# One subtraction on GpSimd, one exponential and one sum in place of eight exponentials, in the compressed branch of a two-layer decoder

## The chip, the cores and the metric

The kernel runs on one core of a Trainium2 chip. Its engines run side by side, each through a queue of its own, in order: TensorE (PE in the profile; PEld is its loading of weights), VectorE (DVE), ScalarE (ACT), GpSimd (POOL) and SyncE (SP), which issues the transfers. An instruction that needs another engine's result waits on a semaphore, and what stands behind it in its queue waits too. The metric is device time in microseconds (us), as the median of several runs.

## The reference, cut to what matters

Layer 1 is native sparse attention. Its compressed branch lets each of 16 heads (4 groups of 4) attend to 63 compressed key blocks; the probabilities also choose which blocks the second branch reads.

```python
    lg_c = jnp.einsum('bsgrd,bcgd->bgrsc', q, kc).astype(jnp.float32) * scale
    mask_c = cmp_end[None, :] <= pos[:, None]
    p_c = jax.nn.softmax(jnp.where(mask_c, lg_c, NEG), axis=-1)
    p_c = jnp.where(mask_c, p_c, 0.0)
    o_c = jnp.einsum('bgrsc,bcgd->bsgrd', p_c.astype(vc.dtype), vc)
    ...
    imp = jnp.einsum('bgsc,cj->bgsj', p_c.sum(axis=2), overlap)
    ...
    imp = jnp.where(forced, FORCE, jnp.where(causal, imp, -1.0))
    _, idx = lax.top_k(imp, n_sel)
```

## The kernel before, in words

The sequence of 1024 positions is cut into eight tiles of 128. Layer 0 comes first, then the projections of layer 1, with which the compressed branch is interleaved, then the attention of layer 1 and the output layer.

The compressed branch is worked in 16 units, here called unit 0 to unit 15 in their order. A unit (`cmp_unit`) is one group of four heads by two tiles of positions, so it has eight rows of 64 scores on each of 128 partitions. `cmp_main` walks through nine steps; step n issues the two units of a group g and half s (n = 2g + s), and between them the transposes (`ptc`) and value matmuls (`oc`) of the step before. The score matmuls of a unit (L1043) write the tile `sc`, of which there is one; VectorE adds the mask and the two halves of the scores (L1052, L1053), and from then on `sc` is free for the next unit. The scores are negated, so VectorE takes minima (L1054) where a softmax takes maxima. ScalarE makes eight exponentials (L1056), one for each row, since each row has its own bias; each also gives the row's sum. VectorE takes reciprocals (L1057). In the first half (s = 0) they are multiplied by the gate (L1068) and GpSimd applies them (L1070). In the second half VectorE normalizes (L1063), sums over heads (L1066), GpSimd applies the gate (L1070), and VectorE chooses blocks in small steps on 128x32 elements (L1074 to L1081).

The names of units in the queues are `cL_s_u`, `cP_s_u`, `cs_s_u`: unit 0 is `0_0`, unit 1 `0_1`, unit 2 `1_0`, unit 3 `1_1`, and the next group begins again.

`merge` runs this main line together with a filler, the projections that are left (`nsa_fill`, `nsa_zs`: the tiles `pn_v`, `pn_ka`, `pn_kr`, `nz`): after a piece of the main line it takes pieces of filler by their stated costs. That sets the order on TensorE. Each section of weights comes in by a transfer, VectorE makes its high part (`whi`, L128) and GpSimd the low part (`wlo`, L129, 128x1024). The transposes' results are split by ScalarE (`pth`, L147) and VectorE (`ptl`, L148). On the other engines the order is set by the scheduler of the program builder, which sees the dependences; it is fixed when the kernel is built.

Of the kernel before, what the change touches and what calls it, by code (L numbers as in the profile page):

```python
# [13 lines left out]
AF = mybir.ActivationFunctionType  # L14
OP = mybir.AluOpType
AX = mybir.AxisListType
# [5 lines left out]
P = 128  # L22
# [18 lines left out]
def tile_fox_nsa(ctx, tc, a, out):  # L41
    nc = tc.nc
    V, A, G, T = nc.vector, nc.scalar, nc.gpsimd, nc.tensor
# [993 lines left out]
    def cmp_unit(g, s, u, Q):  # L1037
        nm = f"{g}_{s}_{u}"
        kcm = ready["kcm"]
        sc = psC.tile([P, 2, 512], F32, tag="sc", name=f"sc_{nm}")  # L1040
        for y in range(2):
            for r in range(4):
                T.matmul(sc[:, y, r * P:(r + 1) * P], Q[r][:, (2 * u + y) * P:(2 * u + y + 1) * P],  # L1043
                         kcm[:, g].rearrange("p a c -> p (a c)"), start=True, stop=True)
        sc = sc.rearrange("p y (r a c) -> p y r a c", r=4, a=2)
        t0 = 4 * s + 2 * u
        L = pc[0].tile([P, 2, 4, 64], F32, tag="cL", bufs=2, name=f"cL_{nm}")
        Pc = pc[0].tile([P, 2, 4, 64], F32, tag="cP", bufs=4, name=f"cP_{nm}")
        sm = pc[0].tile([P, 3, 8], F32, tag="cs", bufs=3, name=f"cs_{nm}")
        L8 = L.rearrange("p y r c -> p (y r) c")  # L1050
        P8 = Pc.rearrange("p y r c -> p (y r) c")
        V.tensor_tensor(L, sc[:, :, :, 1, :], cmask[:, t0:t0 + 2, None, :].to_broadcast([P, 2, 4, 64]), OP.add)  # L1052
        V.tensor_tensor(L, sc[:, :, :, 0, :], L, OP.add)  # L1053
        V.tensor_reduce(sm[:, 0, :], L8, AX.X, OP.min)  # L1054
        for i in range(8):
            A.activation(P8[:, i, :], L8[:, i, :], AF.Exp, bias=sm[:, 0, i:i + 1], scale=-1.0, accum_out=sm[:, 1, i:i + 1])  # L1056
        V.reciprocal(sm[:, 2, :], sm[:, 1, :])  # L1057
        if t0 == 0:
            V.tensor_scalar(sm[:, 2, 0:4], sm[:, 2, 0:4], crow, None, OP.mult)
        ri = sm[:, 2, :].rearrange("p (y r) -> p y r", y=2)  # L1060
        gc = gates[:, t0:t0 + 2, 12 * g:12 * g + 12:3]
        if s:
            V.tensor_tensor(P8, P8, sm[:, 2, :, None].to_broadcast([P, 8, 64]), OP.mult)  # L1063
            pcs = pc[0].tile([P, 2, 65], F32, tag="pcs", bufs=2, name=f"pcs_{nm}")
            G.memset(pcs[:, :, 0:1], 0.0)
            V.tensor_reduce(pcs[:, :, 1:65], Pc.rearrange("p y r c -> p y c r"), AX.X, OP.add)  # L1066
        else:
            V.tensor_tensor(ri, ri, gc, OP.mult)  # L1068
            gc = ri
        G.tensor_tensor(Pc, Pc, gc[:, :, :, None].to_broadcast([P, 2, 4, 64]), OP.mult)  # L1070
        if s:
            im = pc[0].tile([P, 2, 16], F32, tag="im", bufs=2, name=f"im_{nm}")
            mx = pc[0].tile([P, 2, 8], F32, tag="mx", bufs=2, name=f"mx_{nm}")
            V.tensor_reduce(im, pcs[:, :, 1:65].rearrange("p y (j c) -> p y j c", c=4), AX.X, OP.add)  # L1074
            V.tensor_tensor(im, im, pcs[:, :, 0:64:4], OP.add)
            V.tensor_tensor(im, im, impt[:, 0, 2 * u:2 * u + 2, :], OP.mult)
            V.tensor_tensor(im, im, impt[:, 1, 2 * u:2 * u + 2, :], OP.add)
            for y in range(2):
                V.max(mx[:, y, :], im[:, y, :])
                V.match_replace(im[:, y, :], mx[:, y, :], im[:, y, :], -2.0)  # L1080
            V.tensor_scalar(selb[:, g, 2 * u:2 * u + 2, :], im, -2.0, BIG, OP.not_equal, OP.mult)  # L1081
        return Pc

    def cmp_main():
# [17 lines left out]
        for n in range(9):  # L1102
            cur = []
            if n < 8:
                g, s = divmod(n, 2)
                yield lambda g=g: ("q", g // 2) in ready and "gates" in ready
                if n == 0:
                    Qs[n] = [load_q(pc[0], r, 0, 8) for r in range(4)]
                    yield 2500
                cur.append(cmp_unit(g, s, 0, Qs[n]))  # L1110
                yield 900
# [3 lines left out]
            if n < 8:  # L1115
                cur.append(cmp_unit(g, s, 1, Qs.pop(n)))
                if n < 7 and ("q", (n + 1) // 4) in ready:
                    Qs[n + 1] = [load_q(pc[0], 4 * ((n + 1) // 2) + r, (n + 1) % 2, 8) for r in range(4)]
                yield 900
                if n < 7 and n + 1 not in Qs:  # L1120
                    yield lambda n=n: ("q", (n + 1) // 4) in ready
                    Qs[n + 1] = [load_q(pc[0], 4 * ((n + 1) // 2) + r, (n + 1) % 2, 8) for r in range(4)]
# [76 lines left out]
    bias = []  # L1199
# [264 lines left out]
```

## Time and profile before

| what | value |
|---|---|
| median of 3 runs | 1553.28 us (1551.8 to 1553.96) |
| the profiled execution | 1553.53 us |
| its span in the profile | 1551.7 us |
| mean granted TensorE clock | 0.967 |
| TensorE busy | 1434.4 us (92%) |
| VectorE busy | 1063.7 us (69%) |
| ScalarE busy | 803.3 us (52%) |
| GpSimd busy | 556.5 us (36%) |
| score matmuls of the compressed branch | 837.3 to 966.5 us |

A profile is one execution; its times count from the start of the span. Busy time is the time with an instruction at work, and idle time is put down to what ended it. The compressed branch takes about a tenth of the span.

### The profile page before, as it was taken

To read this page: it belongs to the slowest core of one execution; us is meant where nothing else is said; L and a number is where in the kernel's file an instruction comes from. 1 tells how busy PE (TensorE), PEld (TensorE's weight loads), DVE (VectorE), ACT (ScalarE), POOL (GpSimd) and SP (SyncE) were. 2 spreads that over 40 slices of the span, in tenths; PEclk is the share of its full clock that TensorE was granted. 3 is DMA by queue.
4 is the path that set the end of the run, shared out by engine and by line. 5 is a ranking of instruction groups with operands and counts; after the bars stand their busy time and mean duration, and the time that the engine had idled before them with its cause. 6 is when DMAs were issued, how large, how long until landed. Compare 5 with 4: busy or idle time off the path is not lost.

```text
span 1551.7 us, 29460 instructions
## 1 busy us (share of the span) xinstructions
PE 1434.4 (92%) x10488; PEld 1188.4 (77%) x10488; DVE 1063.7 (69%) x2756; ACT 803.3 (52%) x2025; POOL 556.5 (36%) x604
## 2 busy tenths in 40 slices
PE   5999999999999787999999979899898998888898
PEld 4888888888787666878888768687787877667686
DVE  6586878778787755457364687787686777678433
ACT  5364646545555643233133655566565666567321
POOL 1232323222233500043241342557647657345300
PEclk9999999999999889999999999999999999899899
DMA  7796767867878756343345586757756856674642
GB/s 263 223 183 146 163 155 156 172 160 149 178 156 174 166 104 231 95 133 96 126 134 176 149 202 179 206 123 151 168 122 143 195 118 137 151 167 113 161 138 95
DMA packets 405763, 242.72 MB, mean 156 GB/s; under 512 B 332464, under 2 KB 353840, under 8 KB 405360
## 3 DMA queue, kind: packets, MB, share of 16 engines
q1 hardware_dynamic: 405616, 240.84, 63.5%
q8 instruction: 83, 1.36, 0.4%
q14 instruction: 64, 0.52, 0.1%
HBM read 120.96 MB, written 44.11 MB: 106 GB/s over the span
## 4 chain that ended last, share of the span: by engine, by line
PE 61%; DVE 16%; ACT 6%; DMA 6%; POOL 6%; issue 4%; SPq 1%; POOLq 0%; DVEq 0%; ACTq 0%
PE S_n L1256 4%; DVE P_n L1263 3%; PE y L133 3%; PE y L135 3%; PE y L134 3%; POOL hl_n L1270 3%; PE ptp_n L1288 2%; PE v L133 2%; PE v L135 2%; PE v L134 2%; PE S L579 2%; PE S L580 2%; PE q L133 2%; PE O L613 2%; PE k L133 2%
## 5 line engine op out<-in xcount | busy, mean ns | idle before, releaser
L1266 ACT ACTIVATE P_n<-P_n,m_n 128x640 f32<-128x640 f32 (+7 forms) x256 | 187.0, 731 | 74.6 <-DVE m_n L1265 37.3
L1256 PE MATMUL S_n<-nk,nq 128*128 128x320 f32 (+5 forms) x768 | 189.0, 356 | 19.4 <-DVE m_n L1263 18.6
L597 ACT ACTIVATE P<-P,m 128x512 f32<-128x512 f32 (+1 forms) x192 | 116.9, 610 | 133.2 <-DVE m L588 132.3
L568 POOL TENSOR_TENSOR Bd<-B,tri 128x128 f32<-128x128 f32 x128 | 62.3, 501 | 245.3 <-DVE m L588 228.5
L1263 DVE CUSTOM_DVE_ANT_0 P_n<-S_n,wmask 128x128 f32<-128x128 f32 (+1 forms) x192 | 113.5, 598 | 53.4 <-POOL hl_n L1270 37.7
L1256 PEld LDWEIGHTS S_n<-nk,nq 128*128 128x128 f32 x768 | 125.2, 194 | 32.3 <-DVE m_n L1263 23.3
L1270 POOL TENSOR_TENSOR hl_n<-P_n,hl_n 128x640 f16<-128x640 f32 (+4 forms) x128 | 141.5, 1109 | 7.5
L599 DVE SCALAR_TENSOR_TENSOR hl<-P,hl 128x512 f16<-128x512 f32 (+1 forms) x192 | 124.1, 664 | 21.8 <-ACT hl L598 20.7
L150 ACT ACTIVATE pth_n<-ptp_n 128x512 f16<-128x512 f32 (+1 forms) x160 | 86.6, 546 | 76.1 <-PE ptp_n L1288 75.4
L1288 PE MATMUL ptp_n<-ident,P_n 128*128 128x128 f32 x576 | 98.2, 292 | 19.3 <-DVE ptl_n L151 10.3
L151 DVE SCALAR_TENSOR_TENSOR ptl_n<-ptp_n,pth_n 128x512 f16<-128x512 f32 (+1 forms) x160 | 100.5, 634 | 20.8 <-ACT pth_n L150 20.1
L1269 POOL CAST hl_n<-P_n 128x640 f16<-128x640 f32 (+4 forms) x128 | 74.1, 584 | 98.7 <-ACT P_n L1266 78.4
L133 PE MATMUL y<-wo,ohi 128*128 128x512 f32 x240 | 96.8, 403 | 8.0 <-ACT ohi L693 8.0
L1288 PEld LDWEIGHTS ptp_n<-ident,P_n 128*128 128x128 f32 x576 | 71.3, 149 | 33.1 <-DVE ptl_n L151 11.9
L134 PE MATMUL y<-wo,ohi 128*128 128x512 f32 x240 | 96.0, 400 | 0.0
L135 PE MATMUL y<-wo,olo 128*128 128x512 f32 x240 | 94.9, 398 | 0.9 <-DVE olo L694 0.9
L598 ACT ACTIVATE hl<-P 128x512 f16<-128x512 f32 (+1 forms) x192 | 92.5, 513 | 4.3 <-DMA pT<-hl 2.8
L1296 PE MATMUL O_n<-nv,pth_n 128*128 128x64 f16 x576 | 76.1, 199 | 3.7 <-ACT pth_n L150 3.7
L579 PE MATMUL S<-KH,Q 128*128 128x512 f32 (+1 forms) x192 | 68.8, 372 | 10.6 <-DVE m L588 10.4
L1297 PE MATMUL O_n<-nv,pth_n 128*128 128x64 f16 x576 | 74.9, 197 | 0.0
L1298 PE MATMUL O_n<-nv,ptl_n 128*128 128x64 f16 x576 | 72.2, 197 | 0.0
L1296 PEld LDWEIGHTS <-pth_n 128*128 128x128 f16 x576 | 53.8, 101 | 21.4 <-ACT pth_n L150 9.1
(384 smaller groups left out, 4517.0 us busy)
## 6 DMA issues: line engine op xcount, KB each, us to landing
nq<-qD SPq DMA_DIRECT2D x64, 256.0 KB
B<-cD SPq DMA_DIRECT2D x16, 512.0 KB
wo<-wD SPq DMA_DIRECT2D x16, 512.0 KB
nq<-qD SPq DMA_DIRECT2D x64, 128.0 KB
of<-oF SPq DMA_DIRECT2D x12, 512.0 KB
x<-in_x_dram SPq DMA_DIRECT2D x8, 512.0 KB
wst_k<-in_fox_w_dram SPq DMA_DIRECT2D x8, 512.0 KB
wst_v<-in_fox_w_dram SPq DMA_DIRECT2D x8, 512.0 KB
```

What stands on the lines that cost most here:

```text
L133: T.matmul(ps, wh, mh, start=first, stop=False, **kw)
L134: T.matmul(ps, wh, ml, start=False, stop=False, **kw)
L135: T.matmul(ps, wl, mh, start=False, stop=last, **kw)
L151: V.scalar_tensor_tensor(lo[:, 0:n], pt[:, 0:n], scale, h, OP.mult, OP.subtract)
L597: A.activation(L[:, 0:n], L[:, 0:n], AF.Exp, bias=init, scale=-1.0, accum_out=self.lr[:, col + c:col + c + 1])
L599: V.scalar_tensor_tensor(lo[:, cs], L[:, 0:n], UP, hi[:, cs], OP.mult, OP.subtract)
L1256: T.matmul(ps[:, b, 0:w], self.q[x][:, qi * P:(qi + 1) * P], k[:, k0 + b * w:k0 + b * w + w], start=(x == 0), stop=(x == 1))
L1263: V.tensor_tensor_reduce(dst, src, mk, 1.0, 3e38, OP.add, OP.min, m)
L1266: A.activation(L, L, AF.Exp, bias=m, scale=-1.0, accum_out=self.l[:, y, qi:qi + 1])
L1270: G.tensor_tensor(hl[:, n:2 * n], L, hl[:, 0:n], OP.subtract)
L1288: T.transpose(pt[:, (x + i) * P:(x + i + 1) * P], L[:, kb * P - k0:(kb + 1) * P - k0], ident)
L1296: T.matmul(o, hi, v[:, 0:64], start=first, stop=False)
```

## The change

In each unit GpSimd subtracts the minima from all eight rows in place, in one instruction whose second operand is the minimum spread over 64 elements; ScalarE then makes one exponential of 128x512 elements, without bias and without sums; and VectorE makes the sums of the rows in one reduction. The rest of the program text is the same.

```diff
         V.tensor_reduce(sm[:, 0, :], L8, AX.X, OP.min)
-        for i in range(8):
-            A.activation(P8[:, i, :], L8[:, i, :], AF.Exp, bias=sm[:, 0, i:i + 1], scale=-1.0, accum_out=sm[:, 1, i:i + 1])
+        G.tensor_tensor(L8, L8, sm[:, 0, :, None].to_broadcast([P, 8, 64]), OP.subtract)
+        A.activation(P8, L8, AF.Exp, scale=-1.0)
+        V.tensor_reduce(sm[:, 1, :], P8, AX.X, OP.add)
         V.reciprocal(sm[:, 2, :], sm[:, 1, :])
```

The program is one line longer, so lines from 1055 on have a number one higher in the changed kernel: the subtraction is L1055, the exponential L1056, the sum L1057, the reciprocal L1058.

TensorE's queue stays as it was but for two matmuls of a projection that change places with three value matmuls. The queues of VectorE, ScalarE and GpSimd are laid anew by the scheduler in the stretch of the 16 units.

VectorE's queue at units 0 and 1, before:

```order
L1054 TENSOR_REDUCE cs_0_0_9013<-cL_0_0_9011 128x8
L1052 TENSOR_TENSOR cL_0_1_9054<-sc_0_1_9045,cmask 128x512
L1053 TENSOR_TENSOR cL_0_1_9054<-sc_0_1_9045,cL_0_1_9054 128x512
L1057 RECIPROCAL cs_0_0_9013<-cs_0_0_9013 128x8
L1054 TENSOR_REDUCE cs_0_1_9056<-cL_0_1_9054 128x8
L1059 TENSOR_SCALAR cs_0_0_9013<-cs_0_0_9013,crow 128x4
L1068 TENSOR_TENSOR cs_0_0_9013<-cs_0_0_9013,gates 128x8
L1052 TENSOR_TENSOR cL_1_0_9100<-sc_1_0_9091,cmask 128x512
```

And the same place in the changed kernel:

```order
L1054 TENSOR_REDUCE cs_0_0_9013<-cL_0_0_9011 128x8
L1057 TENSOR_REDUCE cs_0_0_9013<-cP_0_0_9012 128x8
L1058 RECIPROCAL cs_0_0_9013<-cs_0_0_9013 128x8
L1060 TENSOR_SCALAR cs_0_0_9013<-cs_0_0_9013,crow 128x4
L1069 TENSOR_TENSOR cs_0_0_9013<-cs_0_0_9013,gates 128x8
L1052 TENSOR_TENSOR cL_0_1_9049<-sc_0_1_9040,cmask 128x512
L1053 TENSOR_TENSOR cL_0_1_9049<-sc_0_1_9040,cL_0_1_9049 128x512
L1054 TENSOR_REDUCE cs_0_1_9051<-cL_0_1_9049 128x8
L1057 TENSOR_REDUCE cs_0_1_9051<-cP_0_1_9050 128x8
```

The additions of unit 1 stood ahead of the reciprocal of unit 0; now the sum, the reciprocal and the products of unit 0 stand ahead of them.

VectorE's queue between units 2 and 3 (`im` and `selb` are the small steps that choose the blocks of unit 2), before:

```order
L1074 TENSOR_REDUCE im_1_0_9120<-pcs_1_0_9116 128x32
L1052 TENSOR_TENSOR cL_1_1_9186<-sc_1_1_9177,cmask 128x512
L1075 TENSOR_TENSOR im_1_0_9120<-im_1_0_9120,pcs_1_0_9116 128x32
L1053 TENSOR_TENSOR cL_1_1_9186<-sc_1_1_9177,cL_1_1_9186 128x512
L128 CAST whi_nv_8979<-wst_nv_8977 128x1024
L1076 TENSOR_TENSOR im_1_0_9120<-im_1_0_9120,impt 128x32
L1054 TENSOR_REDUCE cs_1_1_9188<-cL_1_1_9186 128x8
L1077 TENSOR_TENSOR im_1_0_9120<-im_1_0_9120,impt 128x32
```

And the same place in the changed kernel:

```order
L1078 TENSOR_TENSOR im_1_0_9105<-im_1_0_9105,impt 128x32
L1080 MAX mx_1_0_9106<-im_1_0_9105 128x8 x2
L1081 MATCH_REPLACE im_1_0_9105<-mx_1_0_9106,im_1_0_9105 128x16 x2
L1082 TENSOR_SCALAR selb<-im_1_0_9105 128x32
L1052 TENSOR_TENSOR cL_1_1_9171<-sc_1_1_9162,cmask 128x512
L1053 TENSOR_TENSOR cL_1_1_9171<-sc_1_1_9162,cL_1_1_9171 128x512
L128 CAST whi_nv_8979<-wst_nv_8977 128x1024
L1054 TENSOR_REDUCE cs_1_1_9173<-cL_1_1_9171 128x8
L1057 TENSOR_REDUCE cs_1_1_9173<-cP_1_1_9172 128x8
```

Unit 3's additions were spread through the small steps of unit 2; now they stand behind the last of them.

GpSimd's queue at units 2 and 3, before:

```order
L1070 TENSOR_TENSOR cP_1_0_9101<-cP_1_0_9101,gates 128x512
L1065 MEMSET pcs_1_0_9510 128x2
L129 TENSOR_TENSOR wlo_nv_8980<-wst_nv_8977,whi_nv_8979 128x1024
L1070 TENSOR_TENSOR cP_1_1_9187<-cP_1_1_9187,gates 128x512
L1065 MEMSET pcs_1_1_9596 128x2
```

And in the changed kernel:

```order
L1055 TENSOR_TENSOR cL_1_0_9090<-cL_1_0_9090,cs_1_0_9092 128x512
L1071 TENSOR_TENSOR cP_1_0_9091<-cP_1_0_9091,gates 128x512
L1066 MEMSET pcs_1_0_9475 128x2
L129 TENSOR_TENSOR wlo_nv_8980<-wst_nv_8977,whi_nv_8979 128x1024
L1055 TENSOR_TENSOR cL_1_1_9171<-cL_1_1_9171,cs_1_1_9173 128x512
L1071 TENSOR_TENSOR cP_1_1_9172<-cP_1_1_9172,gates 128x512
```

The new subtraction of unit 3 stands behind the low part of the weights whose high part VectorE makes just ahead of unit 3's minimum.

## Rows read from the trace of the kernel before

**Rows 1.** The page, part 1: busy us, share of the span, instructions, by engine.

```profile
PE 1434.4 (92%) x10488; PEld 1188.4 (77%) x10488; DVE 1063.7 (69%) x2756; ACT 803.3 (52%) x2025; POOL 556.5 (36%) x604
```

**Rows 2.** Windows of the stage: busy us and instructions by engine, clock, DMA.

```profile
core 0: us, PE busy (x) PEld busy (x) DVE busy (x) ACT busy (x) POOL busy (x), PEclk, DMA share, GB/s
838.00:931.00 93.00, 80.71 (x399) 65.66 (x397) 66.21 (x146) 59.14 (x225) 32.69 (x27) 0.96 0.66 176
931.00:985.00 54.00, 52.02 (x250) 42.78 (x250) 40.14 (x100) 27.02 (x116) 17.43 (x16) 0.97 0.63 182
```

**Rows 3.** Waits from 833 to 985 us: total us, times, longest us.

```profile
DVE cs L1057 <- ACT cP L1056: 26.2, 12, 3.8
...
PE sc L1043 <- DVE cL L1053: 7.2, 3, 4.8
...
PE oc_c L133 <- ACT pth_c L147: 3.5, 2, 1.9
```

**Rows 4.** Durations: groups by line, and L1070's own (ns, min/median/max).

```profile
L1056 ACT ACTIVATE cP<-cL,cs 128x64 f32<-128x64 f32 x128 | 42.7, 335 | 22.8 <-DVE cs L1054 22.8
L1056 ACT ACTIVATION_READ_ACCUMULATOR cP<-cL,cs 128x1 f32 x128 | 24.0, 187 | 0.0
...
L597 ACT ACTIVATE P<-P,m 128x512 f32<-128x512 f32 (+1 forms) x192 | 116.9, 610 | 133.2 <-DVE m L588 132.3
...
L1070 POOL TENSOR_TENSOR cP<-cP,cs x8: 1042/1044/1356, 845.0 to 957.9; 128x512 f32<-128x512 f32 x8
```

**Rows 5.** Timeline, units 0 to 2: start us, us, engine, line.

```profile
842.75 0.69 DVE L1053 TENSOR_TENSOR cL<-sc,cL 128x512 f32<-128x512 f32 x1
...
844.66 0.17 DVE L1068 TENSOR_TENSOR cs<-cs,gates 128x8 f32<-128x8 f32 x1
...
845.00 1.04 POOL L1070 TENSOR_TENSOR cP<-cP,cs 128x512 f32<-128x512 f32 x1 [8.63 <-DVE cs L1068]
...
848.11 0.69 DVE L1054 TENSOR_REDUCE cs<-cL 128x8 f32<-128x512 f32 x1
...
851.63 0.20 DVE L1057 RECIPROCAL cs<-cs 128x8 f32<-128x8 f32 x1 [2.83 <-ACT cP L1056]
```

**Rows 6.** Timeline of VectorE and GpSimd, units 3 and 4.

```profile
854.90 0.69 DVE L1052 TENSOR_TENSOR cL<-sc,cmask 128x512 f32<-128x512 f32 x1
...
862.62 1.05 POOL L1070 TENSOR_TENSOR cP<-cP,gates 128x512 f32<-128x512 f32 x1 [3.17 <-DVE pcs L1066]
...
862.83 0.92 DVE L1075 TENSOR_TENSOR im<-im,pcs 128x32 f32<-128x32 f32 x1
...
865.03 2.38 POOL L129 TENSOR_TENSOR wlo_nv<-wst_nv,whi_nv 128x1024 fp32r<-128x1024 f32 x1 [1.06 <-PE ptc_c L1097]
...
865.40 2.06 DVE L1081 TENSOR_SCALAR selb<-im 128x32 f32<-128x32 f32 x1
...
868.59 0.69 DVE L1053 TENSOR_TENSOR cL<-sc,cL 128x512 f32<-128x512 f32 x1
```

**Rows 7.** Timeline of TensorE: matmuls of the branch, with what ended a wait.

```profile
844.58 1.00 PE L1043 MATMUL sc<-kcm,nq 128*128 128x128 f32 x8
...
864.39 1.03 PE L1097 MATMUL ptc_c<-ident,cP 128*128 128x128 f32 x8
...
906.51 1.08 PE L1043 MATMUL sc<-kcm,nq 128*128 128x128 f32 x8 [1.10 <-DVE cL L1053]
...
930.44 1.94 PE L1043 MATMUL sc<-kcm,nq 128*128 128x128 f32 x8 [4.83 <-DVE cL L1053]
...
973.85 0.50 PE L133 MATMUL oc_c<-pth_c,vb 128*128 128x512 f32 x1 [1.27 <-ACT ob_c L1131]
```

**Rows 8.** Timeline of VectorE and GpSimd, units 6 to 10.

```profile
883.96 0.69 DVE L1052 TENSOR_TENSOR cL<-sc,cmask 128x512 f32<-128x512 f32 x1 [2.50 <-PE sc L1043]
...
891.26 2.41 POOL L129 TENSOR_TENSOR wlo_nka<-wst_nka,whi_nka 128x1024 fp32r<-128x1024 f32 x1 [8.62 <-PE sc L1043]
...
905.67 0.69 DVE L1053 TENSOR_TENSOR cL<-sc,cL 128x512 f32<-128x512 f32 x1
...
929.62 0.68 DVE L1053 TENSOR_TENSOR cL<-sc,cL 128x512 f32<-128x512 f32 x1
```

## The prediction

> **What bounds the kernel now.** I read the page's busy shares first: TensorE is busy 92% of the span, VectorE 69% [rows 1]. So a change elsewhere moves the time only through a TensorE wait. The change touches one stretch, units 0 to 15 of the compressed branch, from 838 to 985 us. Cut there, the profile shows two halves [rows 2]: up to 931 us TensorE is idle for 93.0 - 80.7 = 12.3 us, after it for only 2.0. The wait table of the stage [rows 3] shows who waits. Eight of these idle microseconds belong to the score matmuls (7.2), which wait for VectorE's second addition, L1053, because there is one score buffer, and 3.5 to value matmuls that wait for ScalarE. VectorE itself stands 26.2 us at its reciprocal, waiting for the eight exponentials. The reader is to see that VectorE, not ScalarE, is the engine that holds TensorE up here: the longest stop, 4.83 us at 930.44, ends when L1053 of unit 10 ends at 930.30 [rows 7, 8]. What decides is therefore how VectorE's queue gets from unit 0 to unit 10.
>
> **The new link, priced.** Removed per unit: eight exponentials of 0.335 us and their accumulator reads [rows 4]; overlapped, they keep VectorE idle 2.83 us between the end of the minimum and the reciprocal where nothing else delays them, as in unit 2 [rows 5]. Added: on GpSimd a subtraction of the shape of L1070, 1.04 us in the median and 1.36 at most [rows 4]; on ScalarE one 128x512 exponential, which layer 0 has at 0.61 us (that row also feeds an accumulator); on VectorE a 128x8 reduction like the minimum, 0.69 [rows 5]. The start behind VectorE takes GpSimd 0.17 us (844.83 to 845.00) [rows 5], and I take 0.04 for each of the two other hand-overs. So the sum starts 0.17 + 1.04 + 0.04 + 0.61 + 0.04 = 1.9 us after the minimum and ends 2.6 after it. As a chain that is 0.2 us shorter than the 2.83 of before. ScalarE gives back some 2.2 us per unit.
>
> **Where it goes wrong.** VectorE takes its instructions in the order of the queue. Before, the additions of the next unit and other work stood between minimum and reciprocal; now the sum stands directly behind the minimum in ten units of sixteen, and all that follows waits with it. So 2.6 us per unit become serial. I replay the queue with the durations of before, dependent instructions 0.72 us apart for the 128x512 ones.
>
> Part A, units 0 to 4. The minimum of unit 0 ends at 840.43 as before; its sum ends at 843.0; reciprocal and two products, 0.7 us, end at 843.7. Unit 1's additions, which ended at 843.44 [rows 5], end at 845.1, and TensorE's scores of unit 2, due at 844.58 [rows 7], start 0.8 us late. Unit 1's minimum ends at 845.8, its sum and products at 848.9; unit 2's minimum ends at 851.0 (848.80 before) [rows 5], its sum at 853.6. Two low-part subtractions, reciprocal, product and the sum over heads (1.4 + 0.2 + 0.7 + 1.1) lead to 857.0, and the selection steps to 859.6. Only then does unit 3 start, at 854.90 before [rows 6]: 4.7 us late. Its additions, a cast of weights and the minimum lead to 862.45. GpSimd has the 2.4 us low part of those weights ahead of the new subtraction, until 864.3; subtraction 865.4, exponential 866.0, sum 866.7, reciprocal, product, sum over heads 868.8, and L1070 runs to 870.0 instead of 863.67 [rows 6]. TensorE's transposes of unit 3, the second half of the 864.39 row [rows 7], wait for it: 5.2 us late. VectorE's next steps end at 874.9: one is held by L1070 as L1075 was (0.92 us), one by the next weights as L1081 was (2.06) [rows 6]. Unit 4's additions end at 876.2 instead of 869.28, and the scores of unit 5 start 6.9 us late. The bounds: with the small steps overlapped as before it is 0.8 + 4.5 = 5.3, and 7.5 if GpSimd takes 1.36 us, its longest L1070.
>
> One rule bears on this. An instruction of VectorE is stretched until a running GpSimd instruction ends: L1081 took 2.06 us from 865.40, inside the GpSimd row from 865.03 to 867.41 [rows 6], though it has only 128x32 elements. The Trainium skill, "SBUF — State Buffer", section "Who interferes with whom", says that the pair of ports is an exclusive lock, which a VectorE step needs that has two SBUF inputs (while GpSimd reads) or runs in a two-port mode, and a reduction never. Taken alone it would charge up to 1.04 us to each of sixteen new subtractions, 17 us; in ten of them VectorE has nothing to run, by its order, so that the sum takes the lock only where other steps stand in between.
>
> Part B, units 5 to 8, in the clock of before. Unit 5 costs nothing: its products end near 881.7, and the additions of unit 6 wait for scores until 883.96 anyway (2.50 us) [rows 8]. From there: minimum 886.1, sum 888.7, two subtractions and a reciprocal 890.3, product and sum over heads 892.1. The cast of the next weights now follows that sum, so that their GpSimd step, at 891.26 beside harmless work before [rows 8], comes behind L1070 and holds the selection to 895.7. Unit 7's additions end at 898.0, its minimum 898.8, sum 901.4, sum over heads 903.45, selection and cast 905.8, the last selection step behind GpSimd 908.3, scale steps 908.9, additions of unit 8 910.35 instead of 906.36 [rows 8]. The scores of unit 9 are 4.0 us later still. Without the GpSimd hold it is 1.5.
>
> Part C, units 9 to 10. In unit 9 three rotary steps stand between minimum and sum, so nothing waits for the link, but one of them is held about a microsecond by the subtraction. ScalarE is earlier, which gives back 0.2 us in parts B and C at the value matmuls. L1053 of unit 10 ends 0.8 us later than the shift so far, and TensorE meets it at the 4.83 us stop.
>
> Part D, units 10 to 15. TensorE has no slack to recover in, 52.0 of 54.0 us. VectorE slips by 2.2 us at units 10 and 11 (two sums, two holds and a longer wait) and keeps it; TensorE feels it first in units 13 and 15, whose L1070 or exponentials come later: the value matmul at 973.85 waits for the copy that stands behind unit 15's exponential [rows 7], and the transposes after it for L1070. I take 2.3; bounds 0 (all of it in VectorE's slack) and 3.
>
> Sum: 6.9 + 4.0 - 0.2 + 0.8 + 2.3 = 13.8. The profiled execution took 1553.53 us beside a span of 1551.7, and the median of the runs shown is 1553.28; 13.8 on it is 1567.1. The attention that follows begins later by the same amount, with nothing seen to take it up. The bounds together: 5.3 + 1.5 - 0.5 + 0 + 0 = 6.3 and 7.5 + 4 + 1.3 + 3 = 15.8; new stops of several microseconds may also lower TensorE's clock, as after 930.44, where eight score matmuls took 1.94 us against 1.08 at 906.51 [rows 7]: up to 3 more.
>
> **Rivals.**
> First, only part A comes true: the later holds fall beside idle time. That is 5 to 9 us, 1560.5. For it speaks that half of the later terms depends on a hold of GpSimd meeting one VectorE step.
>
> Second, faster. The link is 0.2 us shorter, ScalarE gets 35 us back, and TensorE's stops behind ScalarE are 3.5 + 1.3 = 4.8 us with the output copies [rows 3, 7]. If VectorE's longer queue stays inside its 26.2 us of waiting, these vanish: 1548.5. It decides at the transposes of unit 3: they had about 1.1 us of slack (863.67 against 864.8, some 0.4 us into their row), so the four sums before them would have to cost less than that together; the replay gives 6.3. The Trainium skill, "Perfetto Trace Analysis", section "Optimizing Scalar/DVE Operations", says that grouping into larger operations helps a saturated engine, with some 93 ns of access overhead each on ScalarE: seven fewer would, as an estimate, save 0.65 us per unit, while the rows give 2.2. ScalarE is busy 59 of 93 us in the first half, so it is not saturated.
>
> Third, no change: the ten sums of the first half, 6.9 us, and their waits, 10 x 1.9 = 19 us, take the place of the waiting that is there, and the rest fits TensorE's idle time. That gives 1553. The total speaks for it, 26.2 us of waiting [rows 3]; against it, that before the waits were partly filled with the next unit's work.
>
> Fourth, the slower clock comes on top: 1570 to 1573.
>
> **How the numbers follow.** Forecast (10 to 17 us more) 0.55; part A alone 0.22; more than 17 us 0.08; no change 0.07; faster 0.08. A difference under 0.2%, 3.1 us, can hardly be told from none here. The range 1558 to 1572 leaves out the faster and unchanged cases and some of the extremes, 2 in 10. Slower 0.85, within 0.2% 0.07, faster 0.08. The likeliest case's own range is 1563.5 to 1570.5.
>
> **What would show it.** The sum's row should have about 1.9 us of idle time ahead of it on ten units, ended by ScalarE; ScalarE busy less by some 55 us with the reads; the transposes of unit 3 waiting 4 to 5 us for L1070, the scores of units 5 and 9 for L1053, more than before; TensorE idle 24 to 27 us in the stage instead of 14.3. Wrong would be: no wait before unit 3's transposes, or GpSimd's subtraction far from 1.04 us.

## The result, and the profile after

The change made the kernel slower: 1565.55 us in the median of four runs (1565.12 to 1566.88), beside 1552.54 us for the kernel before on the same chip (1549.75 to 1553.96). The ratio is 1.0086, with a 95% interval of 1.0071 to 1.0102. The forecast was 1567.1, with a range of 1558 to 1572. Four executions behind the ratios further down (one of the kernel before, one of e4, two of e10) ran 5% to five times as long as the others of the same kernel and are left out of the ratios.

The first part of the page of after, busy time by engine, answers to [rows 1]:

```profile
PE 1437.9 (92%) x10488; PEld 1190.6 (76%) x10488; DVE 1075.3 (69%) x2772; ACT 769.8 (49%) x1785; POOL 575.1 (37%) x620
```

By this part alone the change looks good. ScalarE is relieved of 33 us, VectorE has 12 us more, GpSimd 19 us more, and none of them is near its limit. The time went up all the same, so the reader has to go to the stretch. Its two halves in after, as busy us and instructions by engine, granted clock, DMA share and GB/s, answer to [rows 2]:

```profile
838.00:943.00 105.00, 85.05 (x404) 68.61 (x402) 76.42 (x155) 38.34 (x75) 44.69 (x37) 0.95 0.61 153
943.00:998.00 55.00, 50.72 (x233) 41.66 (x234) 45.73 (x105) 13.36 (x24) 23.93 (x22) 0.92 0.62 176
```

For a sum I cut each profiled execution from the first score matmul of unit 0 to the first score matmul of the attention that follows, and call this the stage. The same view, for the stage of before:

```profile
837.20:981.70 144.50, 130.24 (x637) 106.37 (x637) 106.35 (x245) 84.96 (x339) 50.11 (x43) 0.96 0.65 179
```

and of after:

```profile
838.40:998.60 160.20, 135.97 (x637) 110.40 (x636) 122.50 (x261) 51.69 (x99) 68.63 (x59) 0.94 0.61 162
```

The stage grew by 15.7 us, with the same 637 matmul records. TensorE's idle time in it, stage less busy, went from 14.3 to 24.2 us, so 9.9 us are new waiting. The other 5.7 us are busy time: the mean granted clock fell from 0.96 to 0.94 of the upper of the two levels, 2.4 GHz, which is 130.24 x (0.96/0.94 - 1) = 2.8 us, and 1.4 to 4.2 within the rounding of the two figures; for the rest I have no row. Outside the stage the profiled execution of after is 2.3 us shorter (span 1565.1 less 160.2 against 1551.7 less 144.5).

Who waits for whom in the stage of after, as total us, times and longest us, answers to [rows 3]:

```profile
ACT cP L1056 <- POOL cL L1055: 58.7, 14, 10.3
POOL cL L1055 <- DVE cs L1054: 29.3, 11, 7.5
DVE cs L1057 <- ACT cP L1056: 29.2, 14, 3.9
...
PE ptc_c L1098 <- POOL cP L1071: 8.8, 4, 3.5
...
PE sc L1043 <- DVE cL L1053: 7.2, 3, 5.4
...
PE oc_c L133 <- ACT ob_c L1132: 3.5, 1, 3.5
```

ScalarE now waits for GpSimd, GpSimd for VectorE, and VectorE for ScalarE: the new link, seen from its three ends. VectorE's wait for the exponentials, 29.2 us, is hardly longer than the 26.2 of before. What differs is that work which used to stand ahead of this wait in VectorE's queue now stands behind it. TensorE pays mainly in a place where it paid little before, at the transposes behind GpSimd's gate step: 8.8 us, against three short waits (0.76, 0.34 and 0.44) before.

The link in units 0 and 1, VectorE's, GpSimd's and ScalarE's rows (start us, us, engine, line):

```profile
840.92 0.69 DVE L1054 TENSOR_REDUCE cs<-cL 128x8 f32<-128x512 f32 x1
843.43 0.69 DVE L1057 TENSOR_REDUCE cs<-cP 128x8 f32<-128x512 f32 x1 [1.82 <-ACT cP L1056]
...
844.74 0.69 DVE L1052 TENSOR_TENSOR cL<-sc,cmask 128x512 f32<-128x512 f32 x1
...
841.69 1.04 POOL L1055 TENSOR_TENSOR cL<-cL,cs 128x512 f32<-128x512 f32 x1 [4.14 <-DVE cs L1054]
...
842.77 0.63 ACT L1056 ACTIVATE cP<-cL 128x512 f32<-128x512 f32 x1 [0.55 <-DMA nq<-qD]
```

The minimum ends at 841.61, the subtraction runs to 842.73, the exponential to 843.40, the sum to 844.12: 2.5 us. Unit 1's first addition, which waited only for its scores before, starts at 844.74.

VectorE and GpSimd at unit 3:

```profile
859.82 0.68 DVE L1052 TENSOR_TENSOR cL<-sc,cmask 128x512 f32<-128x512 f32 x1
...
861.75 0.68 DVE L1054 TENSOR_REDUCE cs<-cL 128x8 f32<-128x512 f32 x1
866.06 0.69 DVE L1057 TENSOR_REDUCE cs<-cP 128x8 f32<-128x512 f32 x1 [3.64 <-ACT cP L1056]
...
871.68 2.37 DVE L1082 TENSOR_SCALAR selb<-im 128x32 f32<-128x32 f32 x1
...
861.97 2.40 POOL L129 TENSOR_TENSOR wlo_nv<-wst_nv,whi_nv 128x1024 fp32r<-128x1024 f32 x1 [3.19 <-PE oc_c L135]
864.32 1.04 POOL L1055 TENSOR_TENSOR cL<-cL,cs 128x512 f32<-128x512 f32 x1
868.84 1.05 POOL L1071 TENSOR_TENSOR cP<-cP,gates 128x512 f32<-128x512 f32 x1 [3.48 <-DVE pcs L1067]
...
871.64 2.38 POOL L129 TENSOR_TENSOR wlo_nv<-wst_nv,whi_nv 128x1024 fp32r<-128x1024 f32 x1 [1.51 <-PE ptc_c L1098]
```

Here the subtraction stands behind 2.4 us of other GpSimd work, and VectorE is idle for 3.64 us instead of 1.82. The small step L1082, 0.17 or 0.18 us in five of its eight rows, takes 2.37 here and ends at 874.05, with the second weight step (874.02).

TensorE's rows, the transposes of unit 3, the scores of unit 5, the transposes of unit 7, the scores of units 9 and 11, and the value matmul behind unit 15, answer to [rows 7]:

```profile
869.95 1.46 PE L1098 MATMUL ptc_c<-ident,cP 128*128 128x128 f32 x6 [3.54 <-POOL cP L1071]
...
876.39 1.08 PE L1043 MATMUL sc<-kcm,nq 128*128 128x128 f32 x8 [1.20 <-DVE cL L1053]
...
911.38 1.33 PE L1098 MATMUL ptc_c<-ident,cP 128*128 128x128 f32 x5 [2.68 <-POOL cP L1071]
...
916.96 1.08 PE L1043 MATMUL sc<-kcm,nq 128*128 128x128 f32 x8 [0.52 <-DVE cL L1053]
...
943.09 1.30 PE L1043 MATMUL sc<-kcm,nq 128*128 128x128 f32 x5 [5.45 <-DVE cL L1053]
...
989.99 0.79 PE L133 MATMUL oc_c<-pth_c,vb 128*128 128x512 f32 x1 [3.51 <-ACT ob_c L1132]
```

Measured from the start of the stage, the scores of unit 5 start 5.8 us later than before, those of unit 9 9.3, those of unit 11 11.5, and the attention 15.7. The loss grows at the places that the prediction named.

### The profile page after: what moved, and what is told of

It is laid out like the page before. It is cut to its first block, busy times and chain, and to the rows that moved or that the text cites. A ratio compares the mean times of both kernels' runs of the same rounds, so it can differ in the third digit from the quotient of the medians.

```text
span 1565.1 us, 29255 instructions
## 1 busy us (share of the span) xinstructions
PE 1437.9 (92%) x10488; PEld 1190.6 (76%) x10488; DVE 1075.3 (69%) x2772; ACT 769.8 (49%) x1785; POOL 575.1 (37%) x620
## 5 line engine op out<-in xcount | busy, mean ns | idle before, releaser
L597 ACT ACTIVATE P<-P,m 128x512 f32<-128x512 f32 (+1 forms) x192 | 116.9, 609 | 131.1 <-DVE m L588 130.3
L599 DVE SCALAR_TENSOR_TENSOR hl<-P,hl 128x512 f16<-128x512 f32 (+1 forms) x192 | 123.7, 662 | 20.9 <-ACT hl L598 19.9
```

Source lines behind the costliest of these rows:

```text
L597: A.activation(L[:, 0:n], L[:, 0:n], AF.Exp, bias=init, scale=-1.0, accum_out=self.lr[:, col + c:col + c + 1])
L599: V.scalar_tensor_tensor(lo[:, cs], L[:, 0:n], UP, hi[:, cs], OP.mult, OP.subtract)
```

## The experiments

The theory (T1): VectorE takes its instructions in order, and the way from a unit's minimum to its reciprocal now stands between two units' additions; what lies on that way becomes serial. Two rivals: (R1) GpSimd's sixteen more instructions cost by themselves, by holding VectorE's steps and by standing ahead of GpSimd's other work; (R2) the sums cost, 0.69 us more of VectorE's time in each unit.

All ratios are to the kernel before, timed on the same chip; its median was 1552.54 us beside after, 1553.35 beside e1 to e4, 1554.41 beside e5 to e8 and 1554.57 beside e9 and e10. Stage and idle time are of one profiled execution each, worked out as above.

| kernel | time, us | ratio (95% interval) | stage | TensorE idle |
|---|---|---|---|---|
| before | 1552.54 to 1554.57 | 1 | 144.5 | 14.3 |
| after | 1565.55 | 1.0086 (1.0071 to 1.0102) | 160.2 | 24.2 |
| e1_vsub | 1556.04 | 1.0019 (1.0005 to 1.0034) | 151.9 | 17.1 |
| e2_nosub | 1549.66 | 0.9981 (0.9968 to 0.9994) | 143.0 | 14.4 |
| e3_sum8 | 1553.85 | 1.0007 (0.9987 to 1.0026) | 147.3 | 16.2 |
| e4_force | 1560.3 | 1.0044 (1.0025 to 1.0062) | 153.2 | 20.6 |
| e5_gafter | 1550.38 | 0.9973 (0.9958 to 0.9988) | 142.5 | 13.4 |
| e6_alink | 1563.84 | 1.0059 (1.0043 to 1.0075) | 157.1 | 20.9 |
| e7_sub8 | 1564.73 | 1.0066 (1.0049 to 1.0082) | 158.5 | 23.6 |
| e8_group4 | 1553.14 | 0.9993 (0.9982 to 1.0004) | 146.5 | 16.5 |
| e9_serial | 1562.32 | 1.0044 (1.0026 to 1.0061) | 154.7 | 21.6 |
| e10_group8 | 1549.61 | 0.9964 (0.9948 to 0.998) | 143.3 | 13.6 |

**e1_vsub: the subtraction on VectorE.**

```diff
-        G.tensor_tensor(L8, L8, sm[:, 0, :, None].to_broadcast([P, 8, 64]), OP.subtract)
+        V.tensor_tensor(L8, L8, sm[:, 0, :, None].to_broadcast([P, 8, 64]), OP.subtract)
```

> The changed kernel with the subtraction on VectorE instead of GpSimd; the sum still stands right behind it in VectorE's queue in ten units. Theory (VectorE's queue is made serial by the sum's place): the link from minimum to the end of the sum becomes 0.72 + 0.04 + 0.63 + 0.04 + 0.69 = 2.1 us instead of 2.6, and the three places where the subtraction stands behind other GpSimd work (1.9 us each) go; 5 to 7 us less than the changed kernel, 1559, still 5 to 8 above before. Rival 1 (GpSimd's port lock and queue are the cause): all of the loss goes, 1552 to 1554. Rival 2 (VectorE's added busy time is the cause): twice as much of it, 1570 or more.

It gave back more than three quarters of the loss, and came out between the 1559 of T1 and the 1552 to 1554 of R1, although VectorE has 8.7 us more to do in the stage (131.2 us busy against 122.5). Unit 0, VectorE:

```profile
839.47 0.69 DVE L1055 TENSOR_TENSOR cL<-cL,cs 128x512 f32<-128x512 f32 x1
840.91 0.69 DVE L1057 TENSOR_REDUCE cs<-cP 128x8 f32<-128x512 f32 x1 [0.74 <-ACT cP L1056]
```

The subtraction takes 0.69 us here, follows the minimum without a hand-over, and never stands behind GpSimd's weight steps. So the engine with more work loses less when the way is shorter. That speaks against R2, and does not yet tell T1 from R1.

**e2_nosub: no subtraction.** The exponential takes the scores unshifted, with a scale that keeps it finite, so the minima are left out of the softmax.

```diff
-        G.tensor_tensor(L8, L8, sm[:, 0, :, None].to_broadcast([P, 8, 64]), OP.subtract)
-        A.activation(P8, L8, AF.Exp, scale=-1.0)
+        A.activation(P8, L8, AF.Exp, scale=-1.0 / BIG)
```

> The changed kernel without the subtraction: the exponential takes the scores themselves, scaled by 1e-30 so that all stays finite (it leaves the softmax's minima out of use). Theory: the link is 0.04 + 0.63 + 0.04 + 0.69 = 1.4 us, of which VectorE waits 0.7; before it waited up to 2.83 and filled part of that. Units 0 to 3 cost 4 x 1.4 = 5.6 us against 6.5 of waiting before, so the loss is gone: 1551 to 1555. Rival 2 (added busy time): the sums alone, 11 us, remain, 1558 to 1563. Rival 1 predicts 1552 to 1554 as well, so this run tells rival 2 apart and not rival 1.

A little faster than any of the three expected, and faster than before: the sum on VectorE and the one exponential cost nothing by themselves. Since the exponential does not use the minimum, it runs beside it, so this kernel's way is shorter than any that uses the minima.

**e3_sum8: the sums alone moved to VectorE.** The eight exponentials with their biases, as before, without their sums.

```diff
-        G.tensor_tensor(L8, L8, sm[:, 0, :, None].to_broadcast([P, 8, 64]), OP.subtract)
-        A.activation(P8, L8, AF.Exp, scale=-1.0)
+        for i in range(8):
+            A.activation(P8[:, i, :], L8[:, i, :], AF.Exp, bias=sm[:, 0, i:i + 1], scale=-1.0)
```

> Before with one change: the eight exponentials stay, with their bias and without their sums, and VectorE makes the sums in one reduction. Nothing is added on GpSimd, ScalarE gets nothing back. Theory: 0.69 us more in VectorE's queue per unit behind a wait as long as before, ten units ahead of the stop at unit 10, some of it filled: 3 to 7 us above before, 1556 to 1560. Rival 1 (GpSimd): nothing is lost, 1552 to 1554. Rival 2 (busy time): 11 us or near it, 1561 to 1564.

No difference from before can be measured. T1 had asked for 3 to 7 us and missed; the time is where R1 had put it, so this run counts against T1's price for the sum. VectorE is busy 119.1 us in this stage, 12.8 more than before. R2 falls with this run and e2.

**e4_force: the order of before, in part.** One copy of a single element on VectorE makes the sums of a step's first unit wait for the additions of its second unit; everything behind the sums comes after it.

```diff
+        def back(nxt=None):
+            if nxt is not None:
+                V.tensor_copy(sm[:, 1, 0:1], nxt[:, 0, 0, 0:1])
...
+                back0(L)
+                back1()
```

> The changed kernel with the same instructions on the same engines and one more: a one-element copy by VectorE that ties the sum of a pair's first unit to the additions of its second, so that these stand ahead of that sum. The two links of a pair then overlap. Theory: in units 0 to 3 about 2.5 of the 5.8 us come back, in units 6 and 7 about as much: 4 to 8 us less than the changed kernel, 1558 to 1562. Rivals 1 and 2: the subtractions and the sums are all there, so nothing changes, 1564 to 1567.

As expected, half of the loss came back (1.0086 to 1.0044) and half stayed. TensorE still waits at the transposes for GpSimd's gate step at four places, 1.28 to 3.05 us each; the longest:

```profile
926.32 1.97 PE L1101 MATMUL ptc_c<-ident,cP 128*128 128x128 f32 x8 [3.05 <-POOL cP L1074]
```

So the order on VectorE is a part of the loss. That it is not the whole of it this run does not show, since it does not bring back the order of before: the sums come later yet, and a step's first unit has 5.3 to 13.4 us from its minimum to its reciprocal, where before it had 2.83 to 3.77.

**e5_gafter: the same subtraction, off the way.** Only the order of two lines differs from the change, and the exponential takes the scores unshifted, as in e2.

```diff
+        A.activation(P8, L8, AF.Exp, scale=-1.0 / BIG)
         G.tensor_tensor(L8, L8, sm[:, 0, :, None].to_broadcast([P, 8, 64]), OP.subtract)
-        A.activation(P8, L8, AF.Exp, scale=-1.0)
```

> The subtraction stays on GpSimd, with the same shape, but stands behind the exponential: nothing waits for it on the way from minimum to sum. The exponential takes the scores unshifted, so the minima are left out of the softmax. If the longer way from minimum to sum is what costs (the prediction's theory), this is near the kernel without a subtraction: 1549 to 1554 us, first scores to first attention matmul of the stage 142 to 148 us. If GpSimd's being busy, its hold of VectorE's steps and its queue are what cost, it is near the changed kernel: 1562 us or more, stage 157 us or more. In between, both carry a part, and the place gives the shares.

VectorE's queue is the same as in e2. GpSimd's group in the stage, count, busy us and mean ns, is as busy as in after:

```profile
L1056 POOL TENSOR_TENSOR cL<-cL,cs 128x512 f32<-128x512 f32 x16 | 17.5, 1092 | 34.2 <-DVE cs L1054 18.9 <-ACT cP L1055 14.9 <-DVE im L1076 0.4
```

Sixteen subtractions, 17.5 us of GpSimd, and the time is that of the kernel without them. So R1 does not explain the loss: GpSimd's added work costs nothing that can be measured where nothing waits for its result. VectorE's steps are held here too: it is busy 120.68 us in the stage against 117.07 in e2, 3.6 more, where after has 122.50, 5.4 more. Whether holds at after's own places would be hidden as well, no run shows. The Trainium skill, "SBUF — State Buffer", section "Who interferes with whom", describes the exclusive lock by which single steps of VectorE are held; the trace agrees for single steps (2.37 us for L1082 above, beside a weight step), and this run shows that what sixteen subtractions add to it is hidden.

**e6_alink: the same length on another engine.** No subtraction (the minima are left out as in e2), but two copies of the scores in place on ScalarE.

```diff
-        G.tensor_tensor(L8, L8, sm[:, 0, :, None].to_broadcast([P, 8, 64]), OP.subtract)
-        A.activation(P8, L8, AF.Exp, scale=-1.0)
+        A.copy(L8, L8)
+        A.copy(L8, L8)
+        A.activation(P8, L8, AF.Exp, scale=-1.0 / BIG)
```

> No subtraction (the minima are left out of the softmax), but two copies of the unit's 128x512 scores on ScalarE between minimum and exponential, some 1.2 us that GpSimd has no part in. If the length of the way from minimum to sum costs, by any engine, this is 6 to 13 us above the kernel without a subtraction: 1556 to 1562 us. If only GpSimd's work costs, it is as the kernel without a subtraction: 1548 to 1553 us.

Slower by 0.78% of the time than e2 (1.0059 less 0.9981), 12 us, the upper end of what T1 expected, with GpSimd as free as before. Its rows on ScalarE in unit 0:

```profile
839.27 0.62 ACT L1055 COPY cL<-cL 128x512 f32<-128x512 f32 x1
839.92 0.62 ACT L1056 COPY cL<-cL 128x512 f32<-128x512 f32 x1
840.62 0.63 ACT L1057 ACTIVATE cP<-cL 128x512 f32<-128x512 f32 x1
```

They put some 1.3 us on the way, and they make the exponential wait for the minimum too: from minimum to reciprocal it is 3.97 us in the mean of the sixteen units, against 1.13 in e2. ScalarE is busy 69.7 us in this stage, less than the 85.0 of before, so its load is not the cause. A longer way costs, then, without any part of GpSimd in it.

**e7_sub8: GpSimd's subtraction, and the exponentials of before.** They make the sums too, so VectorE has no new step.

```diff
-        A.activation(P8, L8, AF.Exp, scale=-1.0)
-        V.tensor_reduce(sm[:, 1, :], P8, AX.X, OP.add)
+        for i in range(8):
+            A.activation(P8[:, i, :], L8[:, i, :], AF.Exp, scale=-1.0, accum_out=sm[:, 1, i:i + 1])
```

> The subtraction on GpSimd as in the changed kernel, but the eight exponentials of before behind it, which also make the sums, so that VectorE has no sum of its own. The way from minimum to reciprocal is 1.2 to 1.4 us longer than before. By the prediction's theory the reciprocal comes later, not the next unit's additions where these stand ahead of it: 1557 to 1563 us. If the sum on VectorE were the cost, it would be as before, 1552 to 1555 us.

This was worse than expected, near the changed kernel. The next unit's additions stand ahead of the reciprocal here in part, as before: in unit 0 the first of them runs in the wait. So the sum is not needed for the loss. VectorE waits 39.5 us for the exponentials in this stage:

```profile
DVE cs L1058 <- ACT cP L1057: 39.5, 15, 5.2
```

That is 13.3 us more than before [rows 3], and the stage is 14.0 us longer. The longest of these waits, 5.2 us, is in unit 4, where the subtraction starts 2.1 us after the minimum, behind other GpSimd work, as in unit 3 of after. Without a bias an exponential of 64 elements takes 0.24 us instead of 0.335 [rows 4], so the way from minimum to reciprocal, read off the timeline of all sixteen units, is longer by only 3.66 - 3.13 = 0.53 us in the mean, less than I had put into the expectation. Over sixteen units that is 8.5 us, near the 9.3 us of new idle time; the rest is TensorE's busy time, 4.6 us over that of before.

**e8_group4: two exponentials, no subtraction.** A candidate for a faster kernel: one minimum for the four heads of a tile, given to the exponential as its bias.

```diff
-        V.tensor_reduce(sm[:, 0, :], L8, AX.X, OP.min)
-        G.tensor_tensor(L8, L8, sm[:, 0, :, None].to_broadcast([P, 8, 64]), OP.subtract)
-        A.activation(P8, L8, AF.Exp, scale=-1.0)
+        V.tensor_reduce(sm[:, 0, 0:2], L.rearrange("p y r c -> p y (r c)"), AX.X, OP.min)
+        for y in range(2):
+            A.activation(P8[:, 4 * y:4 * y + 4, :], L8[:, 4 * y:4 * y + 4, :], AF.Exp, bias=sm[:, 0, y:y + 1], scale=-1.0)
```

> One minimum for four heads of a tile, so two exponentials of 128x256 that take it as their bias, no subtraction, the sums on VectorE as in the change. The way from minimum to sum is some 0.3 us longer than with one exponential and nothing on GpSimd. If the subtraction's step was the whole loss, this is 1548 to 1552 us and beats both kernels by a little; if two exponentials cost what the kernel without a subtraction gained, 1552 to 1555 us.

It has the time of the kernel before, as the second of the two cases had it. A softmax needs no minimum of its own row, any shift common to the row will do, so the subtraction is dispensable; two exponentials and a sum are then about as good as eight exponentials with sums.

**e9_serial: the kernel before, only serial.** All of its work is kept; one copy of a single element per unit makes the unit's first addition wait for the reciprocal of the unit before it.

```diff
+        if "sm" in ready:
+            V.tensor_copy(L[:, 0, 0, 0:1], ready["sm"][:, 2, 0:1])
+        ready["sm"] = sm
         V.tensor_tensor(L, sc[:, :, :, 1, :], cmask[:, t0:t0 + 2, None, :].to_broadcast([P, 2, 4, 64]), OP.add)
```

> The kernel before with all of its work, and one copy of a single element per unit on VectorE that makes each unit's first addition wait for the reciprocal of the unit before it; nothing of the change is in it. If what stands between minimum and reciprocal on VectorE decides (the prediction's theory: 2.8 us become serial in about half of the units, those whose next additions had come first, though the selection steps of a unit may still come later), this is 1557 to 1564 us, with the scores of units 5 and 9 waiting longer for the additions. If VectorE's 26 us of waiting could take up a changed order, it is 1552 to 1555 us, and then the loss of the change has to lie in the new steps themselves.

Nothing of the change is in this kernel, and it loses 6.8 us (0.44% of 1554.57, the time of before beside it). VectorE at units 0 and 1:

```profile
839.95 0.69 DVE L1057 TENSOR_REDUCE cs<-cL 128x8 f32<-128x512 f32 x1
843.94 0.20 DVE L1060 RECIPROCAL cs<-cs 128x8 f32<-128x8 f32 x1 [3.31 <-ACT cP L1059]
...
844.71 0.15 DVE L1053 COPY cL<-cs 128x1 f32<-128x1 f32 x1
844.97 0.69 DVE L1055 TENSOR_TENSOR cL<-sc,cmask 128x512 f32<-128x512 f32 x1
```

The 3.31 us stand idle here, and the addition comes at 844.97; before, unit 1's two additions were done by 843.44 [rows 5]. The transposes of unit 3 wait 4.65 us on TensorE, as in after they wait 3.54:

```profile
871.50 1.54 PE L1100 MATMUL ptc_c<-ident,cP 128*128 128x128 f32 x6 [4.65 <-POOL pcs L1068]
```

The copies themselves are 0.15 us each, 2.3 us for fifteen of them, a third of the loss. So most of it is the effect of the order by itself.

**e10_group8: one exponential that takes its shift as a bias.** One minimum for all eight rows of a partition; the first unit of each group (units 0, 4, 8 and 12), in which some rows are masked whole, keeps two minima and two exponentials.

```diff
+        n = 1 if t0 else 2
+        V.tensor_reduce(sm[:, 0, 0:n], L8.rearrange("p (n e) c -> p n (e c)", n=n), AX.X, OP.min)
+        for y in range(n):
+            w = slice(8 // n * y, 8 // n * (y + 1))
+            A.activation(P8[:, w, :], L8[:, w, :], AF.Exp, bias=sm[:, 0, y:y + 1], scale=-1.0)
```

> One minimum and one exponential with it as its bias for all eight rows of a partition (two of each in the first unit, whose first rows are masked whole), no subtraction, the sums on VectorE. The way from minimum to sum is 0.04 + 0.63 + 0.04 us, the shortest of all kernels that use the minima. By the prediction's theory this is between the kernel without a subtraction and that with two exponentials, 1549 to 1553 us, and faster than both kernels of the change. If it were as before or slower, 1553 to 1556 us, what the kernel without a subtraction gained came from its exponentials not waiting for the minimum at all.

As T1 expected, and faster than both kernels of the change: 1549.61 us, ratio 0.9964 to before, and by the two ratios (0.9964/1.0086) 1.2% under after. Unit 1 in this kernel:

```profile
843.49 0.69 DVE L1055 TENSOR_REDUCE cs<-cL 128x1 f32<-128x512 f32 x1
844.97 0.69 DVE L1059 TENSOR_REDUCE cs<-cP 128x8 f32<-128x512 f32 x1 [0.79 <-ACT cP L1058]
...
846.01 0.69 DVE L1052 TENSOR_TENSOR cL<-sc,cmask 128x512 f32<-128x512 f32 x1
```

The sum is still directly behind the minimum, but the wait is 0.79 us instead of 1.82. The longest stop on TensorE is still there and longer, 6.80 us at the scores of unit 11 against 4.83 [rows 7]:

```profile
927.14 1.94 PE L1043 MATMUL sc<-kcm,nq 128*128 128x128 f32 x8 [6.80 <-DVE cL L1053]
```

So the stage as a whole gains only 1.2 us in its profiled execution, of the 5.6 us that the ratio gives (0.36% of 1554.57; 3.1 to 8.1 by its interval). Where the rest comes from, these rows do not show; e10 is a faster kernel, but only the 1.2 us can be laid to the shorter way. A shift shared by eight rows is safe only while their scores lie so near to each other that no row's exponentials all vanish; for other data e8's version is the safer one.

## Why the prediction was right

**The link.** Predicted 1.9 us of wait and 2.6 to the end of the sum; measured 1.82 and 2.5 in unit 0, with a subtraction of 1.04 us. GpSimd's start was 0.08 to 0.15 us in twelve units, and not 0.17. The 0.61 us taken for the exponential was a mean over four shapes; layer 0's 128x512 form, which has a bias and an accumulator, takes 0.71, and the new one without them took 0.63, so this term was near by luck. In eleven units nothing stands between minimum and sum, and VectorE waited ahead of the sum in 14, not ten. ScalarE's busy time fell by 33.5 us, near the 35 that its 2.2 us per unit make, and not by the 55 that it gave as a sign: the reads lay over the short exponentials, so that their own times added up to more than the engine's.

**Part A, 6.9 at the scores of unit 5: measured 5.8.** The scores of unit 2 came 0.5 us late (0.8), unit 3 3.7 (4.7), and the transposes of unit 3 ended 4.8 us late (5.2). The subtraction of unit 3 stood behind the weight step as replayed, and the two holds of small steps came as said, the one through L1071 (0.84 us for the step), the other through the next weights (2.37). Not foreseen was unit 4, where the subtraction stood behind two GpSimd steps of the value projection; the scores of unit 6 are 6.1 us late, so that it cost 0.3.

**Part B, 4.0: measured 9.3 - 5.8 = 3.5.** The hold came where it was expected, behind unit 6. In the timeline a small step of VectorE stands inside GpSimd's weight step:

```profile
900.60 2.29 DVE L1077 TENSOR_TENSOR im<-im,impt 128x32 f32<-128x32 f32 x1
...
900.45 2.39 POOL L129 TENSOR_TENSOR wlo_nka<-wst_nka,whi_nka 128x1024 fp32r<-128x1024 f32 x1
```

**Parts C and D, 0.8 - 0.2 + 2.3 = 2.9: measured 2.2 + 4.2 = 6.4.** These were sized too small. Part C, between the scores of units 9 and 11, took 2.2. Of part D's 4.2 us, 2.2 are the value matmul at 989.99, which waits 3.51 us for ScalarE's copy where it waited 1.27 [rows 7]. The place was named: ScalarE starts unit 15's exponential at 988.82, after 5.13 us of waiting for the subtraction, and the copy behind it at 989.36. The mean granted clock of the last 55 us was 0.92; it was 0.97 in the second half before [rows 2].

**What the sum left out.** It counted waiting. In the stage TensorE waits 24.2 us, the lower end of the 24 to 27 that the prediction put there, which is 9.9 more and not 13.8 (its own sum would have asked for 14.3 + 13.8 = 28.1); 5.7 us are matmuls that took longer. Its "eight" idle microseconds at the scores are 7.2 in its own row, and nothing hangs on them. The prediction had the slower clock as its fourth rival, "up to 3 more", on top of the sum; in truth it came with a smaller sum. The stage alone, 15.7 us on 1553.28, would have made 1569.0. So the total was near because errors offset each other: the waiting was put too large and the longer matmuls were left out, parts A and B were too large and C and D too small, and some 2 us went outside the stage. The mechanism and its places were right; that the total came out within 2 us is in part luck. The attention that follows took 566.5 us in the profiled execution of after and 570.0 in that of before. In the profiled executions of the ten experiments it took 566.1 to 570.0, whatever their stages did, so these few us can't be laid to the change.

**The reason itself.** That a serial order costs is shown by e9, with no part of the change; that a longer way costs without GpSimd, by e6; that GpSimd's being busy off the way does not, by e5; that the sums do not, by e3. One thing in the prediction's account is too narrow: it laid the loss to the sum's place directly behind the minimum. e7 has no such sum and loses nearly as much, and e4, with the additions back ahead of the sums, keeps half of the loss. The way's end counts as well as its place: the reciprocal, the gate step and the transposes hang on it. VectorE's rows say how much of each there is. Over the sixteen units the way from the end of the minimum to the start of the reciprocal is 50.0 us before and 52.3 after, so it is hardly longer; but VectorE does other work inside it, the new sum left out, for only 12.2 us after, where it was 20.1. About 10 us more of the way thus hold no other work, beside 9.9 us of new waiting on TensorE. In e9 the same count is 7.0 us, beside 7.3 of new waiting, but in e2 it falls by 15 and TensorE waits no less: a sign of the order's part, and no price. How after's 13 us divide between order and length is not settled: e4 changes other positions with it, e6 and e7 have orders of their own, and the scheduler lays the queues anew for every kernel (only e2 and e5 have the same VectorE queue).

**The rivals.** Part A alone is out: the shift grows to 9.3, 11.5 and 15.7 us behind it. Faster and no change are out for the change as it is; e10 shows that a kernel with one exponential and VectorE's sums can be faster than before once the subtraction is off the way.

The Trainium skill, "Perfetto Trace Analysis", section "Optimizing Scalar/DVE Operations", has beside its advice to group for a saturated engine the reverse one, that engines which are not saturated but cause bubbles elsewhere may gain from smaller pieces. The runs here bear on the first: grouping eight exponentials came with a gain of 0.36% in e10, though ScalarE is not saturated (of it 1.2 us lie in the stage, where the way became shorter, with 0.79 us of wait), and with a loss of 0.86% in the change, where a step on a third engine was put into the way.

## What to carry to other kernels

Price a regrouping by the way from the last input to the first output that others need, over all engines and hand-overs, not by the busy time that it saves: here ScalarE got 33 us back and the kernel lost 13. The way's length alone is not enough: from minimum to reciprocal it grew only from 3.13 to 3.27 us in the mean. Look at what stands behind the new wait in each queue and used to run inside it, and at what stands ahead of the new step in the queue that it joins (here 2.4 us of weights). If a step on another engine is only there to make a grouping possible, look for a form that does without it; here the bias operand with a shared shift did the work of the subtraction.

## What the runs showed of the hardware

An exponential whose bias comes from a tile takes about 0.09 us longer than one with none: 0.72 against 0.63 us for 128x512 (e10 and after), 0.335 against 0.24 us for 128x64 (before and e7). The Trainium skill, "ScalarE: Activation LUTs", section "What ACT_TABLE_LOAD costs", has about 93 ns for each such operand, and the trace agrees.

GpSimd was 17.3 us busier in a stage of 143 us without a measurable loss (e5 beside e2), although VectorE was held for 3.6 us more, and although a single VectorE step of 0.18 us can take 2.37 beside a GpSimd step (L1082 in after). And waiting goes with slower work: where TensorE's idle time in the stage was 20 us or more, its busy time for the same work was 132.6 to 136.2 us, and 128.6 to 131.1 where it was below 17; e1, with 17.1 us idle, had 134.8. That is a coincidence of rows, and no run here changed the idle time alone.
